# A rotary embedding on one core: the first store released by the second row's sum instead of by a product of the third row

## The chip, the core and the metric

The kernel runs on one core of a Trainium2 chip. The metric is the device time of one execution in microseconds (us). Beside the engines VectorE (DVE), ScalarE (ACT), GpSimd (POOL) and SyncE (SP), 16 DMA engines move data between HBM and the on-chip memory; they are given work by queues, of which this kernel uses two: GpSimd's (software_dynamic in the profile) and SP's (hardware_dynamic). TensorE is not used.

## The reference

The input x has shape 8 x 2048 x 16 x 64 (batch, sequence, heads, head size) in fp32; cos and sin have shape 2048 x 32. Neighbouring elements of the last axis form pairs, and each pair is rotated:

```
x1, x2 = x[..., 0::2], x[..., 1::2]
out[..., 0::2] = x1 * cos - x2 * sin
out[..., 1::2] = x1 * sin + x2 * cos
```

The same cos and sin serve all batch rows and all heads. The output is fp32.

## The kernel before, in words

One batch row (2048 x 16 x 64 values, 8.4 MB in fp32) is spread over 128 partitions, 16 sequence positions to a partition, 16384 values each. The work is done in bf16: GpSimd's DMAs turn fp32 into bf16 on the way in and bf16 into fp32 on the way out. The tile xt has five slots of one row each; rows 0 to 4 live in slots 0 to 4, and rows 5, 6 and 7 in slots 0, 1 and 2 again (HOME). So row 5 can be loaded when row 0 has been stored, and rows 6 and 7 when rows 1 and 2 have.

The order on every engine is the order in which the program is written (manual_schedule); the semaphores that keep data in order are put in by the language from what each instruction reads and writes. The parts are:

- Loads. SP loads the first quarter of row 0 as fp32 (L101), and ScalarE turns it into bf16 (L108). GpSimd issues the DMAs for sin (L102), cos (L103), the rest of row 0 (L104), rows 1 and 2 as one DMA, and rows 3 and 4 as one DMA (load, L70). Later it issues the load of row 5 and that of rows 6 and 7, also from L70.
- Tables. VectorE builds the tables s_tab (sin, -sin in turn) and c_tab (each cos twice), L110 to L112.
- rotate, three VectorE instructions for a row: the first product qt = x * s_tab (L89), the second product x = x * c_tab in place (L92), and the sum x = x + qt with the two elements of each pair of qt swapped (L97). Row 0 is rotated in two parts, a quarter and three quarters; every other row in one.
- Stores. GpSimd issues (store, L74) row 0, rows 1 and 2, rows 3 and 4, and rows 5 and 6. The last row is turned into fp32 by ScalarE in four pieces (L138), into the space of slots 3 and 4 (wide), and stored by SP (L139).

The first store waits for two one-element copies on ScalarE. The first (L120) copies the last element of the third row's first product, qt, into a tile gate that nobody reads; so it waits for that product. The second (L121) copies an element of slot 0 onto itself; the store of slot 0 must wait for it, and ScalarE does it after the first copy. They are called from within rotate(2), between L89 and L92, through the argument between.

After the first store GpSimd copies one element of slot 4 into a tile mark (L126), which makes it wait until rows 3 and 4 are loaded. Then it issues the store of rows 1 and 2 (L127, by L74; it waits for row 2's sum), the load of row 5 (it waits until row 0 is stored), the load of rows 6 and 7 (it waits until rows 1 and 2 are stored), and, after rows 3 and 4 are rotated, their store.

Of the kernel before, what the change touches and what calls it, by code (L numbers as in the profile page):

```python
# [2 lines left out]

# [4 lines left out]


@with_exitstack  # L10
def kernel(
    ctx: ExitStack,
    tc: tile.TileContext,
    x: bass.AP,
    cos: bass.AP,
    sin: bass.AP,
    out: bass.AP,
):
    nc = tc.nc
    fp32 = mybir.dt.float32  # L20
    bf16 = mybir.dt.bfloat16
    mult = mybir.AluOpType.mult
    add = mybir.AluOpType.add

    B, S, H, D = x.shape
    P = 128
    K = S // P
    KP = 16
    D2 = D // 2
    HD = H * D  # L30
    NX = 5
    HEAD = 4
    PART = 4
    STAGE = 3


    HOME = [0, 1, 2, 3, 4, 0, 1, 2]

    x_t = x.rearrange("b (p k) h d -> b p k (h d)", p=P, k=K)
    out_t = out.rearrange("b (p k) h d -> b p k (h d)", p=P, k=K)  # L40
    x_r = x.rearrange("b (p k) h d -> p b (k h d)", p=P, k=K)
    out_r = out.rearrange("b (p k) h d -> p b (k h d)", p=P, k=K)
    cos_t = cos.rearrange("(p k) c -> p (k c)", p=P, k=K)
    sin_t = sin.rearrange("(p k) c -> p (k c)", p=P, k=K)

    consts = ctx.enter_context(tc.tile_pool(name="consts", bufs=1))
    stage = ctx.enter_context(tc.tile_pool(name="stage", bufs=1))

    xt = consts.tile([P, NX, K * HD], bf16)
    cos_sb = consts.tile([P, K * D2], fp32)  # L50
    sin_sb = consts.tile([P, K * D2], fp32)
    c_tab = consts.tile([P, K, D], bf16)
    s_tab = consts.tile([P, K, D], bf16)

    wide = (
        xt[:, STAGE : STAGE + 2]
        .rearrange("p a c -> p (a c)")
        .bitcast(fp32)
        .rearrange("p (k c) -> p k c", c=HD)
    )  # L60

    gate = consts.tile([1, 1], bf16)
    mark = consts.tile([1, 1], bf16)

    def home(b, k0=0, k1=K):
        return xt[:, HOME[b], k0 * HD : k1 * HD].rearrange("p (k c) -> p k c", c=HD)

    def load(b, n):
        h = HOME[b]
        nc.gpsimd.dma_start(out=xt[:, h : h + n], in_=x_r[:, b : b + n])  # L70

    def store(b, n):
        h = HOME[b]
        nc.gpsimd.dma_start(out=out_r[:, b : b + n], in_=xt[:, h : h + n])  # L74

    def rotate(b, k0=0, k1=K, between=None):
        nk = k1 - k0
        xp = home(b, k0, k1)
        qt = stage.tile([P, KP, HD], bf16, name="qt", tag="work")

        def rows(a):
            return a.rearrange("p k (h e) -> p k h e", h=H, e=D)

        def tab(a):
            return dataclasses.replace(
                a, offset=a.offset + k0 * D, ap=[a.ap[0], [D, nk], [0, H], [1, D]]
            )

        nc.vector.tensor_tensor(out=rows(qt[:, :nk]), in0=rows(xp), in1=tab(s_tab), op=mult)  # L89
        if between is not None:  # L90
            between(qt)
        nc.vector.tensor_tensor(out=rows(xp), in0=rows(xp), in1=tab(c_tab), op=mult)  # L92
        q_swap = dataclasses.replace(
            qt, offset=qt.offset + 1, ap=[qt.ap[0], [2, nk * HD // 2], [-1, 2]]
        )
        x3 = xp.rearrange("p k (a j) -> p (k a) j", j=2)
        nc.vector.tensor_tensor(out=x3, in0=x3, in1=q_swap, op=add)  # L97

    with tc.manual_schedule():
        head = stage.tile([P, HEAD, HD], fp32, name="st", tag="work")  # L100
        nc.sync.dma_start(out=head[:, :HEAD], in_=x_t[0, :, :HEAD])  # L101
        nc.gpsimd.dma_start(out=sin_sb, in_=sin_t)  # L102
        nc.gpsimd.dma_start(out=cos_sb, in_=cos_t)  # L103
        nc.gpsimd.dma_start(out=home(0, HEAD), in_=x_t[0, :, HEAD:])  # L104
        load(1, 2)
        load(3, 2)

        nc.scalar.copy(out=home(0, 0, HEAD), in_=head[:, :HEAD])  # L108
        s2 = s_tab.rearrange("p k (i j) -> p (k i) j", j=2)
        nc.vector.tensor_copy(out=s2[:, :, 0], in_=sin_sb)  # L110
        nc.vector.tensor_scalar_mul(s2[:, :, 1], sin_sb, -1.0)  # L111
        nc.vector.tensor_copy(  # L112
            out=c_tab.rearrange("p k (i j) -> p (k i) j", j=2),
            in_=cos_sb.to_broadcast([P, K * D2, 2]),
        )
        rotate(0, 0, HEAD)
        rotate(0, HEAD, K)

        def first_store(qt):
            nc.scalar.copy(out=gate, in_=qt[:1, KP - 1, HD - 1 :])  # L120
            nc.scalar.copy(out=xt[:1, HOME[0], :1], in_=xt[:1, HOME[0], :1])  # L121
            store(0, 1)

        rotate(1)
        rotate(2, between=first_store)
        nc.gpsimd.tensor_copy(out=mark, in_=xt[:1, 4, K * HD - 1 :])  # L126
        store(1, 2)  # L127
        load(5, 1)
        load(6, 2)
        rotate(3)  # L130
        rotate(4)
        store(3, 2)
        for b in range(5, B):
            rotate(b)
            if b == 6:
                store(5, 2)
        for k in range(0, K, PART):
            nc.scalar.copy(out=wide[:, k : k + PART], in_=home(B - 1, k, k + PART))  # L138
        nc.sync.dma_start(out=out_t[B - 1], in_=wide)  # L139


# [1 line left out]
_INS = ['x', 'cos', 'sin']  # L143
_OUTS = [((8, 2048, 16, 64), 'float32')]


# [23 lines left out]
```

## Time and profile before

| what | us |
|---|---|
| median of 3 runs | 316.54 |
| lowest and highest of the 3 | 316.34, 316.61 |
| the profiled execution | 316.21 |
| its span, first to last instruction | 314.4 |
| VectorE busy | 210.4 |
| ScalarE busy | 19.3 |
| GpSimd busy | 12.4 |
| one full-row VectorE instruction (L89, L92, L97) | 8.69 |
| GpSimd queue, share of the 16 DMA engines over the span | 92.0% |
| SP queue, share of the 16 DMA engines over the span | 7.9% |

The span counts from the first to the last instruction; the profiled execution's own time is 1.8 us longer. The views used below are: the page (busy table, a row of 40 slices of the span, and the chain of waits that ended last); the table of windows, which gives for a stretch of time each engine's busy time and the mean busy share of the DMA engines; the timeline, which lists instructions with their start, their duration and, in brackets, how long the engine was idle before and what ended it; and the DMA view, which gives the transfers' time from issue to landing. The bytes in these views are those of the side that is written, so a load shows half the GB/s of a store at the same pace, as its bf16 result is half of what is read. Rows are counted from 0 in the code, so the second row is row 1 and the third is row 2.

### The profile page before, as it was taken

The numbers are of one execution on the slowest core, as the hardware profiler recorded it, in microseconds if no ns is written. First come the engines' busy times: TensorE is split into PE (matmuls) and PEld (weight loads), VectorE is DVE, ScalarE is ACT, GpSimd is POOL, SyncE is SP. The second block draws the span as 40 slices with busy tenths as digits, with TensorE's granted clock in tenths as the row PEclk, the third lists the DMA queues.
The fourth block names the chain that finished last, engine by engine and source line by source line (L and its number), as shares of the span: only waits on it lengthen the run. The fifth ranks groups of instructions, "written<-read, shape, count | busy, mean of one in ns | idle before, by whom it ended". The sixth has DMA issues, their size and how long they took to land.

```text
span 314.4 us, 114 instructions
## 1 busy us (share of the span) xinstructions
DVE 210.4 (67%) x30; ACT 19.3 (6%) x8; POOL 12.4 (4%) x16
## 2 busy tenths in 40 slices
DVE  0549950099999999999992299903999999200000
ACT  1400000000000000000000000000000000790000
POOL 4000000000002500000000000000000000000000
DMA  7999999999999999999999999999999999999996
GB/s 296 238 267 200 200 200 267 200 200 217 250 200 267 459 475 400 400 492 442 400 200 246 221 200 200 250 217 333 400 525 409 400 400 525 409 400 400 525 409 267
DMA packets 2512, 102.24 MB, mean 325 GB/s; under 512 B 208, under 2 KB 208, under 8 KB 336
## 3 DMA queue, kind: packets, MB, share of 16 engines
q0 software_dynamic: 2224, 91.75, 92.0%
q1 hardware_dynamic: 288, 10.49, 7.9%
HBM read 67.63 MB, written 67.11 MB: 429 GB/s over the span
## 4 chain that ended last, share of the span: by engine, by line
DVE 64%; another core or an unknown queue 13%; DMA 7%; ACT 3%; ACTq 1%; issue 0%; POOL 0%; DVEq 0%; PEldq 0%
DVE qt L89 21%; DVE xt L92 21%; DVE xt L97 21%; DMA xt<-in_x_dram 7%; ACT xt L138 3%; ACTq L165 1%; POOL sin_sb L102 0%; POOL cos_sb L103 0%; DVEq L89 0%; DVEq L92 0%; PEldq L165 0%
## 5 line engine op out<-in xcount | busy, mean ns | idle before, releaser
L89 DVE TENSOR_TENSOR qt<-xt,s_tab 128x16384 bf16<-128x16384 bf16 (+2 forms) x9 | 69.7, 7744 | 49.3 <-DMA xt<-in_x_dram 47.0
L92 DVE TENSOR_TENSOR xt<-xt,c_tab 128x16384 bf16<-128x16384 bf16 (+2 forms) x9 | 69.7, 7743 | 0.4
L97 DVE TENSOR_TENSOR xt<-xt,qt 128x16384 bf16<-128x16384 bf16 (+2 forms) x9 | 69.7, 7744 | 0.3
L138 ACT CAST xt<-xt 128x4096 f32<-128x4096 bf16 x4 | 14.1, 3600 | 171.7 <-DVE xt L97 171.7
L74 POOL DMA_DIRECT2D out_dram<-xt x4 | 2.7, 672 | 184.9 <-ACT xt L121 93.5
L110 DVE CAST s_tab<-sin_sb 128x512 bf16<-128x512 f32 x1 | 0.5, 456 | 8.9 <-DMA sin_sb<-in_sin_dram 8.9
L120 ACT COPY gate<-qt 1x1 bf16<-1x1 bf16 x1 | 0.2, 194 | 85.1 <-DVE qt L89 85.1
L126 POOL COPY mark<-xt 1x1 bf16<-1x1 bf16 x1 | 5.0, 5040 | 2.6 <-DMA xt<-in_x_dram 2.6
L70 POOL DMA_DIRECT2D xt<-in_x_dram x4 | 2.7, 694 | 43.2 <-DMA out_dram<-xt 43.2
L108 ACT CAST xt<-st 128x4096 bf16<-128x4096 f32 x1 | 3.6, 3605 | 6.7 <-DMA st<-in_x_dram 6.7
L108 ACT ACT_TABLE_LOAD x1 | 1.3, 1283 | 0.7 <-PEq L154 0.7
L102 POOL DMA_DIRECT2D sin_sb<-in_sin_dram x1 | 0.7, 696 | 0.8 <-PEq L165 0.8
L112 DVE CAST c_tab<-cos_sb 128x1024 bf16<-128x1024 f32 x1 | 0.7, 685 | 0.0
L103 POOL DMA_DIRECT2D cos_sb<-in_cos_dram x1 | 0.6, 569 | 0.0
L104 POOL DMA_DIRECT2D xt<-in_x_dram x1 | 0.6, 557 | 0.0
L111 DVE TENSOR_SCALAR s_tab<-sin_sb 128x512 bf16<-128x512 f32 x1 | 0.4, 445 | 0.0
L121 ACT COPY xt<-xt 1x1 bf16<-1x1 bf16 x1 | 0.2, 188 | 0.0
L154 POOL MEMSET const-float32-0.0<- 128x1 f32 x1 | 0.1, 99 | 0.2 <-issue 0.2
L154 POOL MEMSET const-bfloat16-1.0<- 128x1 bf16 x1 | 0.1, 103 | 0.0
L154 POOL MEMSET const-float32-1.0<- 128x1 f32 x1 | 0.1, 99 | 0.0
L154 POOL MEMSET const-uint8-127<- 128x1 uint8 x1 | 0.1, 99 | 0.0
## 6 DMA issues: line engine op xcount, KB each, us to landing
xt<-in_x_dram POOLq DMA_DIRECT2D x3, 8192.0 KB, 59.4
xt<-in_x_dram POOLq DMA_DIRECT2D x1, 4096.0 KB, 57.6
xt<-in_x_dram POOLq DMA_DIRECT2D x1, 3072.0 KB, 21.2
st<-in_x_dram SPq DMA_DIRECT2D x1, 2048.0 KB, 8.0
sin_sb<-in_sin_dram POOLq DMA_DIRECT2D x1, 256.0 KB, 7.6
cos_sb<-in_cos_dram POOLq DMA_DIRECT2D x1, 256.0 KB, 7.4
out_dram<-xt POOLq DMA_DIRECT2D x4, 49.8
out_dram<-xt SPq DMA_DIRECT2D x1, 30.0
```

The costliest lines, as they stand in the source:

```text
L70: nc.gpsimd.dma_start(out=xt[:, h : h + n], in_=x_r[:, b : b + n])
L74: nc.gpsimd.dma_start(out=out_r[:, b : b + n], in_=xt[:, h : h + n])
L89: nc.vector.tensor_tensor(out=rows(qt[:, :nk]), in0=rows(xp), in1=tab(s_tab), op=mult)
L92: nc.vector.tensor_tensor(out=rows(xp), in0=rows(xp), in1=tab(c_tab), op=mult)
L97: nc.vector.tensor_tensor(out=x3, in0=x3, in1=q_swap, op=add)
L102: nc.gpsimd.dma_start(out=sin_sb, in_=sin_t)
L103: nc.gpsimd.dma_start(out=cos_sb, in_=cos_t)
L108: nc.scalar.copy(out=home(0, 0, HEAD), in_=head[:, :HEAD])
L112: nc.vector.tensor_copy(out=c_tab.rearrange("p k (i j) -> p (k i) j", j=2), in_=cos_sb.to_broadcast([P, K * D2, 2]),)
L126: nc.gpsimd.tensor_copy(out=mark, in_=xt[:1, 4, K * HD - 1 :])
L138: nc.scalar.copy(out=wide[:, k : k + PART], in_=home(B - 1, k, k + PART))
L165: with _tile.TileContext(nc) as tc:
```

## The change

The argument between of rotate goes. The two ScalarE copies and the store of row 0 now stand after rotate(1) and before rotate(2), and the first copy reads the last element of row 1 in xt, which row 1's sum (L97) writes, in place of the last element of qt, which row 2's first product writes. All other instructions and their order on each engine stay as they were.

```diff
-    def rotate(b, k0=0, k1=K, between=None):
+    def rotate(b, k0=0, k1=K):
...
         nc.vector.tensor_tensor(out=rows(qt[:, :nk]), in0=rows(xp), in1=tab(s_tab), op=mult)
-        if between is not None:
-            between(qt)
         nc.vector.tensor_tensor(out=rows(xp), in0=rows(xp), in1=tab(c_tab), op=mult)
...
-        def first_store(qt):
-            nc.scalar.copy(out=gate, in_=qt[:1, KP - 1, HD - 1 :])
-            nc.scalar.copy(out=xt[:1, HOME[0], :1], in_=xt[:1, HOME[0], :1])
-            store(0, 1)
-
         rotate(1)
-        rotate(2, between=first_store)
+        nc.scalar.copy(out=gate, in_=xt[:1, HOME[1], K * HD - 1 :])
+        nc.scalar.copy(out=xt[:1, HOME[0], :1], in_=xt[:1, HOME[0], :1])
+        store(0, 1)
+        rotate(2)
         nc.gpsimd.tensor_copy(out=mark, in_=xt[:1, 4, K * HD - 1 :])
         store(1, 2)
```

## The prediction

> **What bounds the kernel now.** I read the page first: the busy table, the DMA row of the 40 slices and the chain that ended last.
>
> ```profile
> span 314.4 us, 114 instructions
> ...
> DVE 210.4 (67%) x30; ACT 19.3 (6%) x8; POOL 12.4 (4%) x16
> ...
> DMA  7999999999999999999999999999999999999996
> ...
> DVE 64%; another core or an unknown queue 13%; DMA 7%; ACT 3%; ACTq 1%; issue 0%; POOL 0%; DVEq 0%; PEldq 0%
> ```
>
> The chain names VectorE for 64%, but VectorE is busy for only 67% of the span, and the DMA row stands at 9 in every slice but the first and the last. So I cut the span at the moments at which transfers land, and asked for the busy time and the DMA share between them.
>
> ```profile
> core 0: us, DVE busy (x) ACT busy (x) POOL busy (x), PEclk, DMA share, GB/s
> 24.00:62.40 38.40, 19.52 (x3) 0.00 (x0) 0.00 (x0) 1.00 1.01 218
> 62.40:101.10 38.70, 38.43 (x5) 0.29 (x2) 0.56 (x1) 1.00 1.01 230
> 101.10:120.50 19.40, 19.27 (x3) 0.00 (x0) 5.75 (x2) 1.00 1.01 432
> 120.50:159.10 38.60, 38.36 (x6) 0.00 (x0) 0.58 (x1) 1.00 1.02 421
> 159.10:178.40 19.30, 8.24 (x1) 0.00 (x0) 1.42 (x2) 1.00 1.01 217
> 178.40:217.00 38.60, 26.08 (x3) 0.00 (x0) 0.00 (x0) 1.00 1.01 231
> 217.00:255.70 38.70, 38.52 (x5) 0.00 (x0) 0.71 (x1) 1.00 1.01 434
> 255.70:313.50 57.80, 13.63 (x2) 14.12 (x4) 0.00 (x0) 1.00 0.97 417
> ```
>
> The column before the last is the DMA share: about 1.0 in all eight stretches (a packet's time is booked whole, so a little over 1 can stand there). Each stretch is one transfer or pair of rows: loads of rows 1-2 and 3-4, store of row 0, store of rows 1-2, load of row 5, loads of rows 6-7, store of rows 3-4, and the last three rows' stores. Each stretch divided by its rows gives 19.2 to 19.4 us for a row, load or store alike; I take 19.3. Fifteen rows (7 loads, 8 stores) make 289.5 us. Row 0's main load lands at 23.7 (issue at 2.51, 21.2 to landing), and 23.7 + 289.5 = 313.2. The final store is issued at 283.55 and lands 30.0 later, at 313.55. **The 16 DMA engines set the end**, and all the gaps of the queue after 24 us together are 0.35 us, 0.1% of the time. Work on VectorE, ScalarE and GpSimd lies beside it, as long as each transfer is in the queue before the one ahead of it ends.
>
> **The place of the change.** The timeline from 80 to 121 us (start, duration, engine, line):
>
> ```profile
> 79.99 8.69 DVE L97 TENSOR_TENSOR xt<-xt,qt 128x16384 bf16<-128x16384 bf16 x1
> 88.71 8.69 DVE L89 TENSOR_TENSOR qt<-xt,s_tab 128x16384 bf16<-128x16384 bf16 x1
> 97.44 8.69 DVE L92 TENSOR_TENSOR xt<-xt,c_tab 128x16384 bf16<-128x16384 bf16 x1
> 97.44 0.19 ACT L120 COPY gate<-qt 1x1 bf16<-1x1 bf16 x1 [85.09 <-DVE qt L89]
> 97.54 0.19 ACT L121 COPY xt<-xt 1x1 bf16<-1x1 bf16 x1
> 98.02 0.56 POOL L74 DMA_DIRECT2D out_dram<-xt  x1 [93.53 <-ACT xt L121]
> 101.13 5.04 POOL L126 COPY mark<-xt 1x1 bf16<-1x1 bf16 x1 [2.55 <-DMA xt<-in_x_dram]
> 115.15 0.71 POOL L74 DMA_DIRECT2D out_dram<-xt  x1 [8.98 <-DVE xt L97]
> 120.76 0.58 POOL L70 DMA_DIRECT2D xt<-in_x_dram  x1 [4.90 <-DMA out_dram<-xt]
> ```
>
> Today the first product of row 2 (the third row) ends at 97.40, ScalarE's two one-element copies follow, and GpSimd issues the store at 98.02, done at 98.58: 0.62 us from release to issue. The load of rows 3-4 lands at 101.1. The store is thus in the queue 2.5 us before the load ahead of it lands. Whether that is soon enough can be seen in the landings of the five stores and in the packets around the turn:
>
> ```profile
> DMA to landing us min/median/max: 22.5/43.9/88.0
> ```
>
> ```profile
> DMA  0000995000009990000099900000999000005990
> ```
>
> The first line: the least, 22.5, is this store, so it lands at 98.02 + 22.5 = 120.5, which is 19.4 after the load; a row takes 19.3, so the turn from load to store costs 0.1. The longest, 88.0, is the store of rows 3-4, issued at 167.63 while two loads were ahead of it; those land at 216.95 (159.65 + 57.3), it lands at 255.6, 38.7 later, and two rows take 38.6: 0.1 again. The second line is the DMA row from 94 to 106 us in steps of 0.3: bursts of packets begin near 95.2, 97.6, 100.0, 102.4 and 104.8, and the 2.4 us between them does not open where the store takes over.
>
> **The change, part by part.**
>
> Moved: the two copies and the store. They now wait for row 1's sum, which ends at 79.99 + 8.69 = 88.68. With the same 0.62 us the store is issued at 89.30 and done at 89.86, 8.72 us earlier: one VectorE instruction and its gap of 0.03. It brings its one DMA (row 0, 19.3 us of the queue) and passes nothing: on GpSimd the next instruction stays the one-element copy into mark, which waits for the load at 101.13 as before; on SP there is only the last store, at 283.55. Gain at the turn: between 0.0 (the turn at 217, where the store had been queued for 49 us, costs the same 0.1) and 0.1 (the whole turn). I take 0.0.
>
> The second store (L127) waits for row 2's sum, 106.17 + 8.69 = 114.86, in both kernels, and is issued at 115.15, 5.4 us before the first store lands; the load of row 5 waits for the first store's landing. Neither is late or early by the change while the queue serves load and store in turn.
>
> Added wait: ScalarE's gate copy waits for the sum (L97) in place of the product (L89). Behind it on ScalarE are only the second copy and, at 269.4, the casts of the last row. Cost 0. Its source is now slot 1 of xt, which the load of rows 6-7 overwrites, so that load may have one more semaphore to look at. The copy is done 70 us before; the load is issued at 159.65 and its turn comes at 178.4, so 18 us of row 5's load cover it. Cost 0, and with the cover gone a gap of the order of 0.1, since the extra look that row 3's first product takes today, described next, costs 0.06.
>
> Removed: the read of qt by ScalarE, for which row 3's first product had to look. It starts at 114.95, 0.09 after the sum, where other VectorE instructions follow in 0.03. That is 0.06 us of VectorE, hidden by its wait of 11.15 us for row 5.
>
> New company: from 89.86 to 98.58 the store stands in the queue behind 4.7 bursts of the load (11.2 / 2.4), where now nothing stands. The nearest row is the load of rows 6-7: with the store of rows 3-4 behind it for its whole length it took 38.6 (178.4 to 217.0), and the load of rows 3-4 took 38.7 (62.4 to 101.1) with the store behind it only at the end. So the price is between -0.1 and 0.0 by these rows. What they don't show is a store that is queued 4.7 bursts ahead of its turn; as an outer bound I take one lost burst, 2.4 us, and as the value 0.
>
> Sum: 0.0 - 0.0 + 0.0. The profiled execution took 316.21 (314.4 of span and 1.8 around it), so it stays at 316.2; the median of the runs shown is 0.33 higher, 316.54, and for a median I predict **316.5**. About 0.2%, 0.63 us, is what a measurement of this kernel can tell from no change.
>
> **The rivals.**
>
> *The store runs ahead of the load (slower).* Place: mark, ahead of the second store on GpSimd. If packets of the store went between or before those of the load, the load would land later. Mark got through only at 106.17, as VectorE's second product ended at 106.13; I read it as let in between VectorE's instructions. If the load lands by 106.1, nothing changes; by 114.8, mark ends at 114.9 and the second store still leaves at about 115.2. Packet for packet the load would lose 11.2 us and land at 112.3: no loss. The point at which it decides is a loss of 13.7 us: then mark can wait for the next end, 123.6, the second store leaves at 123.9, and the queue is dry from 120.5, for 3.4 us or more. At the far end the whole store overtakes: the load lands at 120.4, mark comes through after row 3's first product at 129.2 (120.5 + 8.7), the second store leaves at 129.5, and 9.1 us are dry. So 319.9 to 325.6. For it: mark's 5.04 us, and that nothing orders the two but the queue. Against: 38.6 us for the load of rows 6-7 with a store behind it. Chance 0.07.
>
> *The longer company costs something (slower).* Up to one burst, 2.4 us, hence 316.5 to 318.9; over 317.2 it counts. Against: the same 38.6. Chance 0.11.
>
> *The first store is late today (faster).* It is issued inside VectorE's second product (97.44 to 106.13). If GpSimd could not write the packets' descriptions until that ended, as mark could not end, the queue would be dry today from 101.1 to 106.1, and the change would free it: its issue lies inside the product that ends at 97.40, 3.7 us before the turn. That gives 316.5 - 5.0 = 311.5. Against: the store landed 19.4 after the load, not 24.3 (5.0 + 19.3), and the bursts show no gap. The Trainium skill, "SBUF — State Buffer", section "SBUF: two separate sides", has this rule: GpSimd is locked out and cannot write descriptors while VectorE runs an instruction in a two-port mode, and the DMA engines idle; its section "Who interferes with whom" takes tensor_tensor out of that and lets it hold up only GpSimd's reads. The trace sides with the second: mark, which reads, took 5.04 us, and the store was not held up. Chance 0.02. A second way to faster is that loads and stores in flight together move more than 19.3 us a row; no stretch shows such a mix, and the two stores that share the engines after 283.55 gain nothing. Chance 0.03.
>
> *The store does not leave earlier.* GpSimd could be held by another wait. Its queue's last known wait for a load ahead of this store ends at 62.4 (23.8 + 38.6), so nothing I see holds it at 89.3. If something did, up to 98, the time is 316.5 too. Chance 0.03.
>
> **How the numbers follow.** Forecast as reasoned 0.74, with 315.9 to 317.1; no earlier issue 0.03, same time; longer company 0.11; overtaking 0.07; faster 0.05. Same: 0.74 + 0.03 = 0.77; slower: 0.18; faster: 0.05. From 315.9 up to 317.1 the range holds 0.77; I carry it to 318.0, half of the way from 317.1 to the 318.9 of a whole lost burst, which adds about half of 0.11 and makes 0.82. Left out are the other half, overtaking, and the faster cases.
>
> **What would show it.** Right: the store's issue near 89.3, its landing still near 120.5 and so some 31.2 us after the issue; load of rows 3-4 at 101.1; mark still at about 101.1 to 106.2, second store at 115.2, stretches of 19.3 us a row. Wrong: the load landing later than 101.3, mark ending after 114.9, a landing of the first store away from 120.5, a stretch with a share under 0.97 between 89 and 160, or rows of another length.

## The result and the profile after

| | before | after |
|---|---|---|
| median, us (9 runs each) | 316.34 | 317.28 |
| lowest and highest | 316.18, 316.61 | 317.05, 317.33 |
| profiled execution, us | 316.21 | 317.33 |
| its span, us | 314.4 | 315.5 |

The changed kernel is slower by 0.9 us: ratio 1.0027, 95% interval 1.0019 to 1.0036. The forecast was no change, 316.5; the change is small, but clear of the noise, and the forecast was wrong.

The timeline of the kernel after, from the end of row 1's sum, without VectorE's lines (its lines L90, L95, L118, L119 and L122 are L92, L97, L120, L121 and L126 of before):

```profile
88.73 0.19 ACT L118 COPY gate<-xt 1x1 bf16<-1x1 bf16 x1 [76.33 <-DVE xt L95]
88.83 0.19 ACT L119 COPY xt<-xt 1x1 bf16<-1x1 bf16 x1
89.31 0.55 POOL L74 DMA_DIRECT2D out_dram<-xt  x1 [84.82 <-ACT xt L119]
102.25 3.94 POOL L122 COPY mark<-xt 1x1 bf16<-1x1 bf16 x1 [12.38 <-DMA xt<-in_x_dram]
115.17 0.70 POOL L74 DMA_DIRECT2D out_dram<-xt  x1 [8.98 <-DVE xt L95]
121.88 0.57 POOL L70 DMA_DIRECT2D xt<-in_x_dram  x1 [6.01 <-DMA out_dram<-xt]
```

The change did what it says: the store is issued at 89.31, 8.71 us earlier. But mark, which waits for rows 3 and 4, starts at 102.25 and not at 101.13: that load lands 1.1 us later. The load of row 5, which waits for the first store's landing, moves by the same 1.1 (120.76 to 121.88). The second store doesn't move.

The table of windows of the kernel after, cut at its own landings (columns as in the prediction: stretch, length, busy times, then DMA share and GB/s):

```profile
24.00:62.40 38.40, 19.57 (x3) 0.00 (x0) 0.00 (x0) 1.00 1.01 218
62.40:102.20 39.80, 39.51 (x5) 0.28 (x2) 0.55 (x1) 1.00 1.01 224
102.20:121.60 19.40, 19.33 (x3) 0.00 (x0) 4.64 (x2) 1.00 1.01 432
121.60:160.40 38.80, 38.56 (x6) 0.00 (x0) 0.57 (x1) 1.00 1.01 419
160.40:179.50 19.10, 6.90 (x1) 0.00 (x0) 1.42 (x2) 1.00 1.02 220
179.50:218.10 38.60, 26.07 (x3) 0.00 (x0) 0.00 (x0) 1.00 1.01 231
218.10:256.80 38.70, 38.50 (x5) 0.00 (x0) 0.70 (x1) 1.00 1.01 434
256.80:314.70 57.90, 13.65 (x2) 14.13 (x4) 0.00 (x0) 1.00 0.97 417
```

One stretch has grown, the load of rows 3 and 4: 38.70 to 39.80. The rest keeps its length (the next two pairs, 38.8 + 19.1 and 38.6 + 19.3, have the same sum). The DMA share of the long stretch is still 1.01, since a packet that takes longer counts as busy for longer: **the share shows that engines have work, not that they move at their pace**. The GB/s, 230 before and 224 now, show it. The DMA row of the kernel after from 94 to 106 us, in steps of 0.3, and the time from issue to landing of its five stores:

```profile
DMA  0000099000000990000000000990000009900000
```

```profile
DMA to landing us min/median/max: 30.0/45.2/89.2
```

Bursts start near 95.5, 97.9, 101.5 and 103.9. The one from 97.9 to 101.5 is the last burst of the load. In the trace's packet records each of its 16 packets takes 3.51 to 3.65 us; in the kernel before they take 2.43 to 2.45. The first store then follows in step. The row of landings no longer has the first store as its least (32.3 after its issue now, 22.5 before).

### The profile page after: what moved, and what is told of

Its sections match the earlier page's. It is cut to its first block, busy times and chain, and to the rows that moved or that the text cites. A ratio compares the mean times of both kernels' runs of the same rounds, so it can differ in the third digit from the quotient of the medians.

```text
span 315.5 us, 115 instructions
## 1 busy us (share of the span) xinstructions
DVE 210.4 (67%) x30; ACT 19.3 (6%) x8; POOL 11.3 (4%) x16
## 4 chain that ended last, share of the span: by engine, by line
DVE 64%; another core or an unknown queue 14%; DMA 7%; ACT 3%; ACTq 1%; issue 0%; POOL 0%; DVEq 0%; PEldq 0%
DVE qt L89 21%; DVE xt L90 21%; DVE xt L95 21%; DMA xt<-in_x_dram 7%; ACT xt L134 3%; ACTq L161 1%; POOL sin_sb L100 0%; POOL cos_sb L101 0%; DVEq L89 0%; DVEq L90 0%; PEldq L161 0%
## 5 line engine op out<-in xcount | busy, mean ns | idle before, releaser
L90 DVE TENSOR_TENSOR xt<-xt,c_tab 128x16384 bf16<-128x16384 bf16 (+2 forms) x9 | 69.7, 7743 | 0.4
L95 DVE TENSOR_TENSOR xt<-xt,qt 128x16384 bf16<-128x16384 bf16 (+2 forms) x9 | 69.7, 7744 | 0.3
L118 ACT COPY gate<-xt 1x1 bf16<-1x1 bf16 x1 | 0.2, 193 | 76.3 <-DVE xt L95 76.3
L122 POOL COPY mark<-xt 1x1 bf16<-1x1 bf16 x1 | 3.9, 3938 | 12.4 <-DMA xt<-in_x_dram 12.4
L119 ACT COPY xt<-xt 1x1 bf16<-1x1 bf16 x1 | 0.2, 188 | 0.0
```

## The experiments

Three words are used throughout. A burst is one packet on each of the 16 DMA engines. A turn is the place in GpSimd's queue where the transfers change from load to store. The lead of a store is the time from its issue to its turn. Where a run's result is given as 316.51 (1.0005, 0.9996 to 1.0015), these are the median time in us, the ratio to the kernel before, and the 95% interval of the ratio.

My theory after the result was only a place: a store that stands in the queue behind the load's last burst slows that burst. Open was why the turn from load to store near 101 us does so, when the one near 217 us, with its store queued 49 us ahead, does not. The first rivals were GpSimd's wait at mark for this very load (M), VectorE's work beside it (V) and the lead with which the store is queued (L); as they fell, others took their place, each named in what was expected. The table sums up what follows; the load's length is from the landing of rows 1 and 2 to that of rows 3 and 4, the burst is the mean of its 16 packets in the profiled execution, and each ratio is to the kernel before on the same chip.

| run | first store issued at | load of rows 3-4, us | its last burst, us | median, us | ratio, 95% interval |
|---|---|---|---|---|---|
| before | 98.0 | 38.6 | 2.44 | 316.34 | 1 |
| after | 89.3 | 39.7 | 3.59 | 317.28 | 1.0027 (1.0019 to 1.0036) |
| nomark | 89.2 | 39.6 | 3.43 | 317.19 | 1.0021 (1.0011 to 1.0030) |
| early44 | 44.2 | 39.6 | 3.43 | 317.24 | 1.0025 (1.0016 to 1.0035) |
| delay97 | 96.8 | 39.6 | 3.26 | 317.17 | 1.0024 (1.0014 to 1.0034) |
| delay98 | 98.1 | 38.7 | 2.45 | 316.26 | 1.0002 (0.9993 to 1.0012) |
| dveidle | 89.4 | 39.6 | 3.02 | 317.37 | 1.0034 (1.0021 to 1.0047) |
| rowmap | 89.7 | 39.5 | 2.90 | 317.30 | 1.0032 (1.0021 to 1.0042) |
| loadsplit | 89.2 | 39.8 | 3.56 | 317.09 | 1.0027 (1.0017 to 1.0037) |
| slots | 89.3 | 39.4 | 3.21 | 317.10 | 1.0022 (1.0012 to 1.0031) |
| smallfirst | 89.2 | 39.6 | 3.44 | 317.27 | 1.0027 (1.0017 to 1.0037) |

**nomark**: GpSimd's copy into mark (L122) is left out.

```diff
-        nc.gpsimd.tensor_copy(out=mark, in_=xt[:1, 4, K * HD - 1 :])
```

> The changed kernel without GpSimd's one-element copy into mark, so that GpSimd waits for row 2's sum, not for the load of rows 3 and 4, while that load's last burst runs. In the changed kernel this load took 39.8 us in place of 38.7, all of the 1.1 us in its last burst. Theory M (GpSimd waiting at mark for this load is what slows its last burst): the load takes 38.7 and the time is that of the kernel before, 316.3. Theory V (VectorE at work while a store stands behind a load's last burst) and theory L (it depends on how long ahead the store is queued): the load keeps 39.8 and the time 317.3.

The last burst stays slow, the time too. GpSimd's wait is not what slows it.

**early44**: the copies and the store stand before rotate(1), and the first copy reads slot 0.

> The changed kernel with the two ScalarE copies and the first store released by row 0's sum, so that the store is issued near 44.2 us, 57 us ahead of its turn and not 12. Theory L (a store queued a few bursts ahead costs, one queued long ahead, as that of rows 3 and 4 is, does not): load of rows 3 and 4 in 38.7, time 316.3. Theories M and V: 39.8 and 317.3, since mark and VectorE are as in the changed kernel.

A store queued 57 us ahead costs as much as one queued 12 us ahead. The lead is not the cause.

**dve217**: in the kernel before, two more VectorE products of row 5 into scratch after rotate(5).

```diff
             rotate(b)
+            if b == 5:
+                for _ in range(2):
+                    extra = stage.tile([P, KP, HD], bf16, name="ex", tag="work")
+                    nc.vector.tensor_tensor(out=four(extra), in0=four(home(5)), in1=whole(s_tab), op=mult)
```

> The kernel before with two more VectorE products of row 5 into scratch after rotate(5), whose result nobody reads, so that VectorE works from 204.6 to 222 us, when the load of rows 6 and 7 ends with the store of rows 3 and 4 long queued behind it; before, VectorE idles there. Theory V: the last burst of this load takes 3.6 us in place of 2.4, the load 39.7 in place of 38.6, the time 317.4. Theories M and L: 38.6, and 316.3, as the 5 us that VectorE is later are hidden by the store of rows 3 and 4 and that of rows 5 and 6.

Rows 6 and 7 took 38.6 us, their last burst 2.4; 316.51 (1.0005, 0.9996 to 1.0015). Its longer span, 315.1, comes from bursts of the first loads, rows 3 and 4 among them (39.5 us); the last section tells of them.

**mark217**: in the kernel before, a second copy into mark after store(3, 2), from slot 2.

> The kernel before with a second one-element GpSimd copy into mark after the store of rows 3 and 4, from slot 2, so that GpSimd waits for the load of rows 6 and 7 while its last burst runs. Theory M: the load of rows 6 and 7 takes 39.7 in place of 38.6 and the time 317.4. Theories V and L: 38.6 and 316.3.

38.6 us; 316.69 (1.0006, 0.9996 to 1.0016). With nomark this rules out GpSimd's wait at both turns.

**dveidle**: VectorE waits for rows 3 and 4 between row 2's two products.

```diff
         nc.vector.tensor_tensor(out=rows(qt[:, :nk]), in0=rows(xp), in1=tab(s_tab), op=mult)
+        if hold:
+            nc.vector.tensor_copy(out=hold_t, in_=xt[:1, 4, K * HD - 1 :])
```

> The changed kernel with a one-element VectorE copy between row 2's two products that reads the last element of slot 4, so that VectorE idles from 97.5 us until rows 3 and 4 have landed. Row 2's sum then ends near 118.8, still ahead of the first store's landing at 120.5, so nothing else should be late. Theory W (VectorE's work beside the last burst slows it at this turn, whatever it was at the later one): load of rows 3 and 4 in 38.7, time 316.3. Theory S (the places in SBUF or HBM that load and store use at this turn, or what stood in the queue before): load in 39.5 or more, time 317.2.

VectorE idles from 97.5 to 102.2, and the last burst still takes 3.0 us, the load 39.6. Theory W falls.

**inplace217**: as dve217, but the second product is in place.

```diff
+                nc.vector.tensor_tensor(out=four(ex), in0=four(home(5)), in1=whole(s_tab), op=mult)
+                nc.vector.tensor_tensor(out=four(ex), in0=four(ex), in1=whole(c_tab), op=mult)
```

> The kernel before with two more VectorE products into scratch after rotate(5), the second in place as row 2's second product is, from about 213.4 to 222.1 us, over the last bursts of the load of rows 6 and 7. Theory W in the form that only a product in place, as the one at work at the first turn, slows the burst: load of rows 6 and 7 in 39.6 in place of 38.6, time 317.3. Otherwise 38.6 and 316.3.

Its timeline has the product in place over the last bursts of the load:

```profile
213.63 8.69 DVE L147 TENSOR_TENSOR ex<-ex,c_tab 128x16384 bf16<-128x16384 bf16 x1
```

38.6 us, burst 2.4; 316.30 (1.0000, 0.9990 to 1.0009). VectorE's work, of either kind, is not the cause.

**split217**: in the kernel before, store(3, 2) becomes store(3, 1) and store(4, 1).

> The kernel before with the store of rows 3 and 4 issued as two stores of one row. Theory O (the turn at 101 us differs from the one at 217 us, which never lost, because its store is of one row): the last burst of the load of rows 6 and 7 takes 3.5 us in place of 2.4, that load 39.7 in place of 38.6, and the time is 317.4. Otherwise 38.6 and 316.3.

38.6 us for rows 6 and 7; 316.26 (0.9999, 0.9990 to 1.0009). The store's rows are not the cause.

**rowmap**: a list ROW = [7, 3, 4, 5, 6, 0, 1, 2] maps the batch rows in all transfers of x and out.

> The changed kernel with the batch rows taken in the order 7, 3, 4, 5, 6, 0, 1, 2 from x and to the output, so that every transfer has the same size, slot and place in the queue but another address in HBM. Theory H (the HBM addresses of this load's end and this store's start matter): load of the fourth and fifth row in 38.7, time 316.3, or a loss at another turn. Otherwise 39.5 or more, and 317.2.

**slots**: other homes in SBUF.

```diff
-    HOME = [0, 1, 2, 3, 4, 0, 1, 2]
+    HOME = [0, 3, 4, 1, 2, 0, 3, 4]
...
-    STAGE = 3
+    STAGE = 1
```

> The changed kernel with other slots: rows 1 and 2 in slots 3 and 4, rows 3 and 4 in slots 1 and 2, rows 5, 6, 7 in slots 0, 3, 4, the last row's fp32 in slots 1 and 2, and rows 5 and 6 stored by two DMAs, since their slots are no longer neighbours. Theory S (the places in SBUF of this load's end and this store's start): rows 3 and 4 land 38.7 after rows 1 and 2, or a loss appears at the turn near 217. Otherwise 39.5 or more, and 317.2.

**loadsplit**: load(3, 2) becomes load(3, 1) and load(4, 1).

> The changed kernel with the load of rows 3 and 4 issued as two loads of one row, so that one transfer more stands in GpSimd's queue ahead of the turn, and the load ahead of the store is of one row. Theory R (where in the queue, counted in packets or transfers from the start, the turn lies): rows 3 and 4 land 38.7 after rows 1 and 2, time 316.3. Otherwise 39.5 or more, and 317.2.

All three keep the slow last burst (2.9, 3.2 and 3.6 us) and the time, and show no loss near 217. HBM addresses, SBUF slots and one transfer more in the queue are not the cause.

**sincos_sp**: cos and sin are loaded by SP's queue.

> The changed kernel with cos and sin loaded by SP's queue, so that GpSimd's queue has two transfers fewer ahead of the turn. Theory R (the loss comes from where in GpSimd's queue, counted in packets from the start, the load's last packet and the store's first one stand): load of rows 3 and 4 in 38.7, and about 1.1 us less than the changed kernel apart from what the start gains or loses. Otherwise its last burst stays at 3.4 to 3.6 us and the load at 39.6 or more.

This one told nothing of its question. SP's small transfers came late beside GpSimd's large ones (sin 31.7 us from issue to landing, 7.6 before; cos 53.6 in place of 7.4), so VectorE started its rows at 55.9, the first store was issued at 109.4, when the load had long landed, and the time was 332.81 (1.0518, 1.0501 to 1.0534).

**firstwrite**: SP stores cos to a part of the last row's output.

```diff
+        nc.sync.dma_start(out=out_t[B - 1, :, 0, : K * D2], in_=cos_sb)
         rotate(0, 0, HEAD)
```

> The changed kernel with a store of cos (0.26 MB, by SP, near 10 us) to a part of the last row's output, which the last store writes over. Theory F (the loss belongs to the first write of the program to HBM): the load of rows 3 and 4 takes 38.7, and the time is 317.3 less 1.1 plus 0.6 for the added 0.26 MB, 316.8. Otherwise the load takes 39.6 or more, and the time is near 317.9.

The load takes 39.4 us, its last burst 3.1; 317.71 (1.0044, 1.0029 to 1.0059), closer to the 317.9 than to the 316.8. That the program has written to HBM before, by another queue, does not take the loss away; the load loses some 0.75 us here and not 1.0.

**smallfirst**: the first store in two DMAs.

```diff
-        store(0, 1)
+        nc.gpsimd.dma_start(out=out_t[0, :, :HEAD], in_=home(0, 0, HEAD))
+        nc.gpsimd.dma_start(out=out_t[0, :, HEAD:], in_=home(0, HEAD))
```

> The changed kernel with the first store cut in two DMAs, a quarter of row 0 (8 KB a partition) and the rest. Theory P2 with one packet read ahead: the loss is the time of the first packet's bytes, 32 KB in the changed kernel (32768 B at the 27 GB/s with which an engine moves a burst's 65536 B in 2.41 us are 1.2 us), so 0.3 us here; load of rows 3 and 4 in 38.9, time 316.6. Otherwise the load takes 39.5 or more, time 317.2.

The loss stays whole with a first packet of a quarter of the bytes. Theory P2, in the form of one packet read ahead, falls.

**between**: GpSimd's queue holds load(1, 2), load(3, 1), store(0, 1), load(4, 1), and mark is left out.

```diff
-        load(3, 2)
+        load(3, 1)
...
+        store(0, 1)
+        load(4, 1)
         rotate(1)
```

> The changed kernel with the first store (released by row 0's sum) between the loads of row 3 and of row 4, and without mark. GpSimd's queue then turns from load to store near 82 us and again near 120.5, where the store of rows 1 and 2, issued at 115, stands behind row 4's last burst. Theory F2: the first turn costs about 1.1 us, the second nothing; time 317.3. Theory D (the loss grows with the time that the queue has only loaded): about 0.9 at the first turn, some 0.3 at the second, where only 19 us of loads lie behind. Theory P2: 1.1 at both; time 318.4.

317.17 (1.0027, 1.0017 to 1.0036). The DMA row of between from 74 to 86 us, then from 112 to 124, both in steps of 0.3:

```profile
DMA  9000000990000009900000000059900000599000
```

```profile
DMA  0000999000005990000059900000599000005990
```

At the first turn the burst that starts near 78.5 is slow: its packets take 3.45 us on average, and row 3 lands 20.3 after rows 1 and 2. At the second turn the bursts keep their step, though the store of rows 1 and 2 was issued at 115.16, before row 4's last burst started. The first turn loses 1.0, the second nothing.

**store62**: a GpSimd store of cos between the two loads.

```diff
         load(1, 2)
+        nc.gpsimd.dma_start(out=out_t[B - 1, :, 0, : K * D2], in_=cos_sb)
         load(3, 2)
```

> The changed kernel with a small GpSimd store of cos (0.26 MB, to a part of the last row's output that the last store writes over) between the loads of rows 1-2 and rows 3-4, so that GpSimd's queue goes from load to store and back near 62 us. Theory F2 (the loss comes once, at the first turn of GpSimd's queue from load to store): rows 1 and 2 land up to 1.1 later, and rows 3 and 4 show no slow last burst; time 317.3 plus 0.6 for the added bytes. Theory P2 (the store's first reads from SBUF take the DMA engine's time from the load's last burst, at any turn that is not covered): the turn near 62 costs little, as 2 KB a partition are read, and the last burst of rows 3 and 4 still takes 3.0 us or more.

Neither as put: the last burst before the small store takes 2.83, the one before the first large store 2.96. 0.4 and 0.5 us are lost, 0.9 in all; 317.56 (1.0037, 1.0024 to 1.0050). A small first store takes a part of the loss, and the next one the rest.

**quarter23**: the first quarter of row 0 is stored ahead of the large loads.

```diff
-        load(1, 2)
-        load(3, 2)
...
+        nc.gpsimd.dma_start(out=out_t[0, :, :HEAD], in_=home(0, 0, HEAD))
+        load(1, 2)
+        load(3, 2)
         rotate(0, HEAD, K)
...
-        store(0, 1)
+        nc.gpsimd.dma_start(out=out_t[0, :, HEAD:], in_=home(0, HEAD))
```

> The changed kernel with the first quarter of row 0 stored by GpSimd as soon as it is rotated, near 20 us, ahead of the loads of rows 1 to 4 in the queue, and the other three quarters where the first store stands. Theory F2 (what is lost, about 1.0 us in all, goes at the first turn from load to store): the load that ends near 24 us is some 1.0 late, and rows 3 and 4 show no slow burst. Theory D (it grows with the time that the queue has only loaded): at most 0.3 near 24 us, and the last burst of rows 3 and 4 still 0.7 or more late. Time 317.3 for both.

Two lines of its timeline, the product that waits for row 0's main load, and mark:

```profile
24.82 6.56 DVE L89 TENSOR_TENSOR qt<-xt,s_tab 128x12288 bf16<-128x12288 bf16 x1 [5.53 <-DMA xt<-in_x_dram]
...
106.89 5.04 POOL L123 COPY mark<-xt 1x1 bf16<-1x1 bf16 x1 [11.27 <-DMA xt<-in_x_dram]
```

The product starts at 24.82 and not at 23.84: 1.0 us is lost at the first turn, 24 us into the run. Rows 1 and 2 land at 68.2, and rows 3 and 4 at 106.9, 38.6 later: nothing is lost at the second, though its store was issued at 95.06. The loss does not grow with the loading before it. The time, 318.29 (1.0060, 1.0046 to 1.0074), has some 1.0 us more than that loss, for another reason: all rows come 5 us later, so the second store is issued only at 120.91, as the queue runs dry, and lands 39.9 us after the first and not 38.6.

**delay97** and **delay98**: the changed kernel with a longer second copy on ScalarE, 9000 elements in delay97 and, as in this cut, 10600 in delay98.

```diff
-        nc.scalar.copy(out=xt[:1, HOME[0], :1], in_=xt[:1, HOME[0], :1])
+        nc.scalar.copy(out=xt[:1, HOME[0], :10600], in_=xt[:1, HOME[0], :10600])
```

> The changed kernel with ScalarE's second copy made 9000 elements long (slot 0 onto itself, one partition), some 7.5 us, so that the first store is issued near 96.8 us, about 1.2 us before the load's last burst starts at 98.0. The theories on GpSimd's wait, on the lead and on VectorE have fallen: the loss was there without mark and with a lead of 57 us, and it was not at the later turn with VectorE at work. Theory P (what counts is whether the store stands in the queue when the load's last burst starts): load of rows 3 and 4 in 39.6 or more, time 317.2. Theory G (the loss shrinks with the time that the store stands there): below 38.9, and 316.4.

> The changed kernel with ScalarE's second copy 10600 elements long, so that its wait, its code and its order stay and only the moment changes: the first store is issued near 98.1 us, as in the kernel before, after the load's last burst has started and before it ends. Theory P (the store must not stand in the queue when the last burst starts): load of rows 3 and 4 in 38.7, time 316.3. If something else of the change were the cause (the source of the gate copy, the code), 39.5 and 317.2.

The store's issue, mark, and the DMA row from 94 to 106 us in delay97:

```profile
96.81 0.56 POOL L74 DMA_DIRECT2D out_dram<-xt  x1 [92.31 <-ACT xt L119]
...
102.12 4.07 POOL L122 COPY mark<-xt 1x1 bf16<-1x1 bf16 x1 [4.76 <-DMA xt<-in_x_dram]
```

```profile
DMA  0000059500000099000000005900000059000000
```

and in delay98:

```profile
98.09 0.55 POOL L74 DMA_DIRECT2D out_dram<-xt  x1 [93.59 <-ACT xt L119]
...
101.12 5.01 POOL L122 COPY mark<-xt 1x1 bf16<-1x1 bf16 x1 [2.48 <-DMA xt<-in_x_dram]
```

```profile
DMA  0000995000009950000009900000099000000990
```

The two differ in the length of that copy, and by it in the moment of the issue, by 1.3 us. Issued at 96.8, 1.4 us before the load's last burst starts near 98.2, the store goes with a slow burst, and the load lands at 102.1; issued at 98.1, 0.2 us after the last burst has started, it does not, and the load lands at 101.1. But for that copy delay98 has the changed kernel's code, and it has the time of the kernel before. So the moment makes the difference, and the boundary lies near the start of the load's last burst.

## Why the prediction was wrong, step by step

- *What bounds the kernel*: right. The end moved by what one stretch of the DMA queue lost, 1.1 us, and by nothing that VectorE, ScalarE or GpSimd did.
- *The moved store*: right in its time (89.30 forecast, 89.31 seen) and in that it passes nothing. The second store stood at 115.17 as forecast.
- *The added wait and the removed read*: right, no cost; row 3's first product starts at 114.91, 0.04 earlier than before, with no effect.
- *The gain at the turn, 0.0 to 0.1*: no gain, as taken.
- *"New company"*: this step failed. I priced a store queued behind a load at 0, from the load of rows 6 and 7, which kept 38.6 us with a store behind it, and kept one lost burst, 2.4 us, as the outer bound. It cost 1.1 us in the profiled execution and 0.9 in the medians, a little under half of that bound. The row I took as nearest is of a later turn, and between and quarter23 show that later turns are free where the first has paid in full (in store62, where it paid 0.4, the next paid 0.5); in the kernel before and in delay98 neither pays. The row for the first turn of the queue from load to store, with a store already behind it, did not exist in the trace of before, and the only row that stood for that turn, 38.7 us with the store issued within the last burst, was on the free side of the very boundary that the change crosses.
- *The rivals*: "the longer company costs something" is what happened, and it had been given a chance of 0.11. The range holds 317.28 only because it was carried on, from 317.1 to 318.0, for this rival; the forecast as reasoned does not hold it. Overtaking did not happen: the store's first packets start at 101.5, behind the load's last ones, and these are longer, not interleaved. The first store was not late before.
- *What would show it*: the load's landing later than 101.3 was named, and came. A share under 0.97, named too, did not come and was no fit sign: the slow burst is booked as busy, and the share stayed at 1.01.

What stays open is what in the DMA path is slow once. Other traffic of the core doesn't show: between 85 and 110 us the packet records of both kernels hold, beside the packets of the load and the store, only 4-byte ones at the load's end. The runs leave this: about 1.0 us is lost at the first turn of GpSimd's queue from load to store if the store is issued well before the load's last burst starts (by 1.2 us in quarter23, by more in the others), wherever that turn lies (24, 82 or 101 us), whatever the slots, the HBM addresses, VectorE and mark; with a small first store, 0.4 there and 0.5 at the next; nothing if the store is issued just after that burst starts.

Where between the two the boundary lies is not settled. In dve217 and mark217, variants of the kernel before, the store was issued 0.72 and 0.55 us ahead of the last burst, and that burst took 2.54 and 2.43 us. But there the loads had already lost some 0.7 us in earlier bursts, as the last section tells, so these runs may have had little left to lose. In firstwrite SP's store came when SP's load had landed; whether a first store that is queued behind a load on SP's own queue pays too was not tried.

## What to carry to other kernels

Where the DMA queue is the bound, an earlier issue is not free by itself: read the lengths from landing to landing, and the step between bursts, not the busy share. A stand-in row for a cost must match in its place in the history of the queue, not only in kind: the first turn from load to store was not like the second. And when a release stands close to a boundary, here 2.5 us ahead of a landing, moving it is best tried in both directions with the moment alone changed, as delay97 and delay98 do.

## What the runs showed of the hardware that was not expected

The first turn's loss itself, above, about 1.0 us once.

In several of the experiments' profiled executions, single bursts of the loads ahead of GpSimd's first store took up to 0.2 us longer than 2.43 (in mark217 those near 57, 62, 67, 69, 72 and 82 us, 2.50 to 2.61), and none after it. So a loss of nearly the same size also comes without an early store: from the landing of row 0's main load to that of rows 3 and 4 dve217 and mark217, with the first store issued at 97.9 and 98.1, took 78.1 us, against 77.3 in the profiled execution of the kernel before and in delay98. This may be what spreads the kernel before, of which no slower run was profiled: 10 of its 111 runs beside the experiments took 316.85 us or more, up to 317.06. No run with an early store took less than 316.85.

The two losses do not simply add up: over the same stretch the table's runs with an early store took 78.2 to 78.6 us, stray bursts or not (after 78.4, nearly all of the loss in the last burst; rowmap 78.6, 0.8 of it in stray bursts and 0.45 in the last one). So it looks as if the early store made certain a loss that the kernel before has in some of its runs only. That the two are one and the same is not shown, and what they share is open.

In sincos_sp SP's transfers of 0.26 MB, beside GpSimd's packets of 2.4 us each, landed 31.7 and 53.6 us after their issue. The Trainium skill, "DMA: Bandwidth & Descriptors", section "Queues, rings and completion order", says that each DMA engine takes turns between its queues packet by packet. The trace agrees: the landings of sin and cos lie 22.4 us apart, 9 packets at 2.5 us, the step that GpSimd's bursts then have, and the packet records show 9 packets of cos on each engine (8 of 2 KB and one of 4 bytes), one to a burst; a queue of small packets gets its turns, but not its share of the bytes.
